# Copies of the first features for feature tiles that follow other work, and weight slots chosen by kind

## The chip, the core and the metric

One core of one Trainium2 chip runs the whole program. The metric is the device time of one execution in microseconds (us). The kernel before took 1661.35 us (median of three runs, 1661.29 to 1663.35).

## What is computed

Two transformer blocks on 256 tokens of width 1024, all in float32. The first is feed-forward, hybrid mixer (attention and a state-space scan), cross-attention on a memory, feed-forward; the second is another mixer and a feed-forward that picks 16 of 16384 experts for each of 8 heads and token.

```python
def first_block(x, mem, ...):
    f = swiglu(rmsnorm(h, ffn1_pre_g[l]), ffn1_w_gu[l], ffn1_w_down[l])
    h = h + 0.5 * rmsnorm(f, ffn1_post_g[l])
    m = hybrid_mixer(rmsnorm(h, mix_pre_g[l]), w_in[l], ...)
    h = h + rmsnorm(m, mix_post_g[l])
    c = memory_cross_attention(rmsnorm(h, xa_pre_g[l]), rmsnorm(mem, mem_g[l]), ...)
    h = h + rmsnorm(c, xa_post_g[l])
    f = swiglu(rmsnorm(h, ffn2_pre_g[l]), ffn2_w_gu[l], ffn2_w_down[l])
    return h + 0.5 * rmsnorm(f, ffn2_post_g[l])
...
def second_block(x, ...):
    proj = rmsnorm_2(x, norm_mix[l]) @ w_in[l]
    ...
    x = x + mix @ w_out[l]
    x = x + peer_ffn(rmsnorm_2(x, norm_ffn[l]), peer_wq[l], peer_keys[l], peer_u[l], peer_v[l])
    return rmsnorm_2(x, norm_f)
```

In `peer_ffn` the kernel multiplies the tokens by all rows of `peer_u`, builds the gates of the chosen experts as dense products of one-hot matrices, and multiplies by all rows of `peer_v`.

## The kernel before

**Units.** All weights come as 533 units of 512 KB, in one fixed list: `ff1` 66 units, `v` 8, `qk` 16, `dt` 1, `xs` 8, `bc` 4, `z` 8, `mk` 8, `wo1` 16, `mv` 8, `xq` 8, `xo` 8, `ff2` 66, `v2`, `g2`, `f2`, `q2` 4 each, `chb` 12, `wo2` 8, `pq` 16, `pu` 128, `pv` 128. SyncE loads a unit into a raw buffer. `prefetch` gives it a slot (a pair of 128x1024 tiles, `hi` and `lo`): ScalarE rounds the raw weights into `hi` (L156), VectorE writes the rest into `lo` (L157). This is called the split of a unit below. Weights and features are both kept as such a pair, so a product is three matmuls, high by high, low by high and high by low. `prefetch` is called from `tick` between pieces of TensorE's work, so a split stands in the queues of ScalarE and VectorE behind whatever was issued before it; the queues are served in order.

**Slots.** There are slots 0 to 3 (`hi0`/`lo0` to `hi3`/`lo3`), slots 4 to 7, and some more pairs taken out of the arenas `ra` and `fa` for a while by `extend`. Of the units in `HELD` each tile holds its weights still (see below); they get the lowest free slot, the others the highest. The addresses of the built program matter for the change: slots 0 to 3 start at 32 modulo 128 bytes; slots 4 to 7, the arenas and the feature buffers `uT` (high and low part) start at 96 modulo 128. In this text a matmul is *level* where its weights and its features have the same residue, and *off* where they are 64 bytes apart.

**Three kinds of matmuls take the units.** `f_tile` (L311, matmuls at L319, L320, L321) holds 128 columns of weights in TensorE and streams the 256 tokens of `uT`, 8 blocks k with three matmuls each; there are 277 such tiles, 6648 matmuls. `half_chunk` (matmuls at L286, L287, L290) and `acc_step` (L336, L338, L340) hold the features and stream 512 columns of weights. An f tile can be broken in its middle: after four blocks `tick` may let other generators put matmuls of attention, scans, transposes or gates in between. The other work is the transposes into `uT` (L397, then ScalarE L402 for the high part, VectorE L406 for the low part), attention (L599 to L636), the scans, and the gates of the experts (one-hot products, L1375) beside the tiles of `pu`.

**Order.** One Python program records all engines' instructions in one order, so each engine's queue follows from the order of the calls; a wait appears where data is needed.

**Where it stands in time** (us from the span's start): `ff1` to 190, first mixer with `v`, `qk`, `xs`, `bc`, `z`, `wo1` to 445, cross-attention to 530, `ff2` to 720, second mixer to 848, `pq` to 905, `pu` 905 to 1305 (gates beside it from 1032), `pv` to the end.

Of the kernel before, what the change touches and what calls it, by code (L numbers as in the profile page):

```python
# [110 lines left out]
class Builder:  # L111
    RAW = 3
    RING = (4, 4)
    VRING = 4

# [3 lines left out]
    def __init__(self, tc, io, dbg=None, stop=None):  # L119
# [11 lines left out]
        self.mm_i = self.sd_i = 0  # L131

# [8 lines left out]
    def prefetch(self, n=1):  # L141
# [130 lines left out]

    def half_chunk(self, u0, t, aT, evac, hook=None):
# [5 lines left out]
        for j in range(4):  # L279
# [3 lines left out]
            for kk in range(2):  # L283
                k = 2 * j + kk
                wh, wl = hi[:, kk * 512:kk * 512 + 512], lo[:, kk * 512:kk * 512 + 512]
                nc.tensor.matmul(ps, ah[:, k, ts], wh, start=(k == 0), stop=False)  # L286
                nc.tensor.matmul(ps, ah[:, k, ts], wl, start=False, stop=False)  # L287
            for kk in range(2):
                k = 2 * j + kk
                nc.tensor.matmul(ps, al[:, k, ts], hi[:, kk * 512:kk * 512 + 512], start=False, stop=(k == 7))  # L290
# [20 lines left out]
    def f_tile(self, u, aT, evac):  # L311

        nc = self.nc
# [14 lines left out]
    def acc_step(self, k, t, w, aT, first, last, halves=range(2)):  # L328
# [6 lines left out]
        for h in halves:  # L335
            nc.tensor.matmul(o[h], ah[:, k, ts], hi[:, hs[h]], start=first, stop=False)  # L336
        for h in halves:
            nc.tensor.matmul(o[h], ah[:, k, ts], lo[:, hs[h]], start=False, stop=False)  # L338
        for h in halves:
            nc.tensor.matmul(o[h], al[:, k, ts], hi[:, hs[h]], start=False, stop=last)  # L340
# [7 lines left out]
    def acc_gemm(self, u0, pairs, n, done=None, mid=None, tail=6, early=1, before_t1=None, have=None):  # L348
# [3 lines left out]
        for i, (aT, k, pos) in enumerate(pairs[:cut]):  # L352
# [3 lines left out]
            for t in range(2):  # L356
                self.acc_step(k, t, w, aT, pos == 0, pos == n - 1)
                if not t:
# [5 lines left out]
        for t in range(2):  # L364
            if t == 1 and before_t1:
                before_t1()
            for i, (aT, k, pos) in enumerate(pairs[cut:], cut):
# [5 lines left out]
                self.acc_step(k, t, self.get(u0 + i), aT, pos == 0, pos == n - 1)  # L373
                if t == 1:
# [14 lines left out]
    def transposes(self, src, t, dst, col=None, kt0=0, n=8, part=None):  # L389
# [4 lines left out]
        for b in range(0, n, 4) if part is None else [4 * part]:  # L394
            ps = self.sd()
            for i in range(4):
                nc.tensor.transpose(ps[:, i * 128:(i + 1) * 128],  # L397
# [79 lines left out]
    def ffn(self, name, row_name, before_t1, done, mid):  # L477
# [4 lines left out]
        if name != "ff1":  # L482
            self.extend(0, 4)
# [21 lines left out]
        def tr(c, ac):  # L505
            ps = self.sd()
            for j in range(2):
                for t in range(2):
                    nc.tensor.transpose(ps[:, j * 256 + t * 128:j * 256 + t * 128 + 128],
# [73 lines left out]
    def attention(self, par, qT, kT, vt, oat, ready):  # L583
# [10 lines left out]
        for j in range(4):  # L594
            while ready[0] <= j:
                yield
            for n in range(2):
                f = 2 * j + n
                nc.tensor.matmul(zv[:, n], kT[rows, f, 0:128], qT[rows, f, :], start=(n == 0), stop=False,  # L599
# [1200 lines left out]
```

## Time and profile before

| | |
|---|---|
| median of three runs | 1661.35 us |
| the profiled execution, its own time | 1661.53 us |
| its span in the trace | 1659.8 us |
| TensorE busy in the span | 1638.8 us, 99% |
| VectorE, ScalarE, GpSimd busy | 69%, 59%, 16% |

All sums below are made against 1661.5 us; the median lies 0.2 us lower. Times in the rows are microseconds from the start of the span. In a timeline row the first number is the start of the instruction, the second its duration; the matmuls overlap, so what one costs is read from the distance of the starts and not from the duration, which is 0.28 us for an f matmul throughout.

### The profile page before, as it was taken

The page shows a single profiled execution, that of the slowest core. Times are in us where ns is not written, and L with a number is a line of the kernel's source. Part 1 is how long each engine was busy: PE and PEld are TensorE (multiplying, and loading weights), DVE is VectorE, ACT ScalarE, POOL GpSimd, SP SyncE. Part 2 cuts the span into 40 slices and gives each one's busy share as a digit, 9 for nine tenths or more (in the row PEclk, how much of TensorE's full clock was granted, in tenths as well). Part 3 has the DMA queues.
Part 4 walks back from the last instruction along what each step waited for, and adds up shares of the span by engine and source line. Part 5 has one row for each costly group of instructions (what it writes and reads, how often), then busy time and mean ns, then how long its engine had stood idle before and what let it go on. Part 6 is the DMA issues. An engine that isn't in the chain of part 4 may idle for free.

```text
span 1659.8 us, 29155 instructions
## 1 busy us (share of the span) xinstructions
PE 1638.8 (99%) x11102; PEld 1490.7 (90%) x11102; DVE 1152.8 (69%) x2366; ACT 980.5 (59%) x1826; POOL 272.3 (16%) x311
## 2 busy tenths in 40 slices
PE   8999999999999999999999999999999999999998
PEld 6999899988898899989889999999999888888886
DVE  7555565777756755567657998899999755555554
ACT  7444476786555644456355564988877554455444
POOL 0000000000000000000100002988888100000000
PEclk9999999999999999999999999999999999999999
DMA  9555443364434755526234555444444555555553
GB/s 332 193 201 190 150 143 128 102 201 148 174 112 165 270 188 201 191 99 196 90 130 153 185 183 190 162 162 167 163 155 162 178 207 198 192 190 195 195 193 127
DMA packets 79325, 288.77 MB, mean 174 GB/s; under 512 B 8784, under 2 KB 8912, under 8 KB 79056
## 3 DMA queue, kind: packets, MB, share of 16 engines
q1 hardware_dynamic: 77904, 281.66, 49.3%
q10 hardware_dynamic: 1280, 5.24, 0.9%
q8 instruction: 87, 1.43, 0.3%
q14 instruction: 54, 0.44, 0.1%
HBM read 285.82 MB, written 1.05 MB: 173 GB/s over the span
## 4 chain that ended last, share of the span: by engine, by line
PE 89%; DVE 6%; issue 2%; ACT 1%; DMA 1%; POOL 0%; SPq 0%; POOLq 0%; DVEq 0%; ACTq 0%
PE mm L319 14%; PE mm L320 14%; PE mm L321 14%; PE acc L336 11%; PE acc L338 11%; PE acc L340 11%; PE mm L290 3%; PE mm L286 3%; PE mm L287 3%; DVE lo L157 2%; PE sd L1375 1%; DVE m L1365 1%; DMA raw<-ws 1%; DVE X L1385 1%; PE sd L397 1%
## 5 line engine op out<-in xcount | busy, mean ns | idle before, releaser
L157 DVE TENSOR_TENSOR lo<-raw,hi 128x1024 fp32r<-128x1024 f32 x419 | 513.7, 1230 | 262.4 <-ACT hi L156 261.2
L319 PE MATMUL mm<-uT,hi 128*128 128x256 f32 x2024 | 576.1, 285 | 3.3 <-ACT fa L1198 1.7
L156 ACT ACTIVATE hi<-raw 128x1024 fp32r<-128x1024 f32 x419 | 442.2, 1058 | 221.5 <-PE acc L340 185.6
L320 PE MATMUL mm<-uT,hi 128*128 128x256 f32 x2024 | 566.4, 280 | 0.0
L321 PE MATMUL mm<-uT,lo 128*128 128x256 f32 x2024 | 566.3, 280 | 0.0
L319 PEld LDWEIGHTS mm<-uT,hi 128*128 128x128 f32 x2024 | 381.5, 189 | 5.7 <-DVE X L1478 2.5
L320 PEld LDWEIGHTS mm<-uT,hi 128*128 128x128 f32 x2024 | 381.7, 189 | 0.8
L321 PEld LDWEIGHTS mm<-uT,lo 128*128 128x128 f32 x2024 | 381.2, 188 | 0.0
L1362 POOL TENSOR_SCALAR m<-iota,kT 128x128 f16<-128x128 f16 x256 | 235.3, 935 | 198.1 <-DVE kT L1345 151.9
L425 POOL TENSOR_TENSOR hr<-hv,mhalf 128x1 f32<-128x1 f32 x26 | 15.2, 585 | 816.4 <-DVE hv L424 816.4
L157 DVE TENSOR_TENSOR lo<-fa,hi 128x1024 fp32r<-128x1024 f32 x74 | 90.1, 1224 | 65.0 <-ACT hi L156 64.3
L338 PE MATMUL acc<-lo,r 128*128 128x512 f32 x336 | 103.5, 389 | 0.0
L336 PE MATMUL acc<-hi,r 128*128 128x512 f32 x336 | 103.4, 389 | 0.0
L340 PE MATMUL acc<-hi,r 128*128 128x512 f32 x336 | 103.4, 389 | 0.0
L156 ACT ACTIVATE hi<-fa 128x1024 fp32r<-128x1024 f32 x74 | 77.4, 1055 | 42.4 <-PE mm L320 23.5
L1475 ACT ACTIVATE X<-mm 128x256 f32<-128x256 f32 (+40 forms) x126 | 39.7, 315 | 99.9 <-PE mm L321 99.0
L1364 ACT ACTIVATE oh<-m,kT 128x128 f16<-128x128 f16 x256 | 81.1, 390 | 0.0
L338 PEld LDWEIGHTS acc<-lo,r 128*128 128x128 f32 x336 | 63.1, 188 | 13.1
L340 PEld LDWEIGHTS acc<-hi,r 128*128 128x128 f32 x336 | 63.1, 188 | 13.1
L336 PEld LDWEIGHTS acc<-hi,r 128*128 128x128 f32 x336 | 63.1, 188 | 13.0
L336 PE MATMUL acc<-hi,ra 128*128 128x512 f32 x216 | 71.0, 410 | 0.6 <-ACT ra L1183 0.6
L338 PE MATMUL acc<-lo,ra 128*128 128x512 f32 x216 | 67.3, 393 | 0.0
(364 smaller groups left out, 2653.2 us busy)
## 6 DMA issues: line engine op xcount, KB each, us to landing
raw<-ws SPq DMA_DIRECT2D x443, 512.0 KB, 3.3
fa<-ws SPq DMA_DIRECT2D x90, 512.0 KB, 3.6
fa<-rows ACTq DMA_DIRECT2D x5, 512.0 KB, 4.1
fa<-mem ACTq DMA_DIRECT2D x1, 1024.0 KB, 7.7
X<-keysT ACTq DMA_DIRECT2D x1, 1024.0 KB, 4.8
out<-X SPq DMA_DIRECT2D x4, 256.0 KB, 2.0
h<-x SPq DMA_DIRECT2D x2, 256.0 KB, 2.8
h<-x SPq DMA_DIRECT2D x1, 512.0 KB, 7.3
```

What stands on the lines that cost most here:

```text
L156: nc.scalar.activation(hi, raw, AF.Copy)
L157: nc.vector.tensor_sub(lo, raw, hi.bitcast(F32))
L286: nc.tensor.matmul(ps, ah[:, k, ts], wh, start=(k == 0), stop=False)
L287: nc.tensor.matmul(ps, ah[:, k, ts], wl, start=False, stop=False)
L319: nc.tensor.matmul(ps, wh, ah[:, k, :], start=(k == 0), stop=False)
L320: nc.tensor.matmul(ps, wh, al[:, k, :], start=False, stop=False)
L321: nc.tensor.matmul(ps, wl, ah[:, k, :], start=False, stop=(k == 7))
L336: nc.tensor.matmul(o[h], ah[:, k, ts], hi[:, hs[h]], start=first, stop=False)
L338: nc.tensor.matmul(o[h], ah[:, k, ts], lo[:, hs[h]], start=False, stop=False)
L340: nc.tensor.matmul(o[h], al[:, k, ts], hi[:, hs[h]], start=False, stop=last)
L1362: nc.gpsimd.tensor_scalar(m1[:, i], self.iota, key(0, i), None, op0=OP.is_equal)
L1364: nc.scalar.activation(oh[:, i], m1[:, i], AF.Copy, scale=key(2, i))
```

## The change

- `f_tile` keeps track of what TensorE did last (`last`: an f tile, other work, or a level token matmul). Where a tile, or the second part of a broken tile, follows something other than an f matmul and its unit is in slots 0 to 3 with `uT` as features, its first blocks take the features from copies instead of `uT`: three blocks after other work, one after a level token matmul. The copies `pr` hold blocks 0 and 1 of the high and low part at residue 32, the residue of slots 0 to 3; for `pq` and `pu` a third copy of the high part of block 2 is added. So six matmuls (eight in `pu`), or three, are level ahead of the off ones.
- `f_tile` issues high by high, low by high, high by low; a tile behind another f tile takes its blocks in the order 3, 4, 5, 6, 0, 1, 2, 7, so that after a break in the middle the copied blocks come next.
- GpSimd writes the copies in `spread`, two small copies for each 128 tokens, behind the writes of `uT`.
- `prefetch` gives units in `HELD` only slots 0 to 3 and the others only slots from 4 on. It takes a slot of the wrong kind only if the unit is fewer than three units ahead of the one in use. Units 4 to 7 of `mv` don't get arena slots. `extend(0, 4)` becomes `extend(0, 3)`; the arena `fa` shrinks from 16768 to 16128 floats for the copies.

```diff
+    AHEAD = 3
...
             slots = [x for x in self.free if x < self.RING[0] or i < FIRST["pq"]]
-            if not slots:
+            if FIRST["mv"] + 4 <= i < FIRST["mv"] + 8:
+                slots = [x for x in slots if x < sum(self.RING)]
+            fit = [x for x in slots if (x < self.RING[0]) == (i in HELD)]
+            if not fit and (i - self.top >= self.AHEAD and i < FIRST["pq"] or not slots):
                 return
-            slot = min(slots) if i in HELD else max(slots)
+            slot = max(fit or slots)
...
+    def level(self, i):
+
+        self.last = "level" if self.slot_of[i] >= self.RING[0] else "other"
...
-        for k in range(8):
+        lead, mine = 0, aT is self.uT and self.slot_of[u] < self.RING[0]
+        todo = list(range(8)) if self.last != "f" else [3, 4, 5, 6, 0, 1, 2, 7]
+        for n, k in enumerate(todo):
+            if self.last != "f":
+                lead = (0 if not mine else 1 if self.last == "level" else 3)
+                self.last = "f"
             wh, wl = hi[:, k * 128:k * 128 + 128], lo[:, k * 128:k * 128 + 128]
-            nc.tensor.matmul(ps, wh, ah[:, k, :], start=(k == 0), stop=False)
-            nc.tensor.matmul(ps, wh, al[:, k, :], start=False, stop=False)
-            nc.tensor.matmul(ps, wl, ah[:, k, :], start=False, stop=(k == 7))
-            if k == 3:
+            xh, xl = ((p[k] if k < lead and k < len(p) else x[:, k, :]) for p, x in zip(self.lead, aT))
+            nc.tensor.matmul(ps, wh, xh, start=(n == 0), stop=False)
+            nc.tensor.matmul(ps, wl, xh, start=False, stop=False)
+            nc.tensor.matmul(ps, wh, xl, start=False, stop=(n == 7))
+            if n == 3:
+                lead = 0
                 self.tick(1.3, False)
...
     def spread(self, hn, t, dst, col):
         self.transposes(hn[t].ap, t, dst, col)
+        ts = slice(t * 128, t * 128 + 128)
+        for p, x in zip(self.pr, dst):
+            self.nc.gpsimd.tensor_copy(p[:, :, ts], x[:, 0:2, ts])
         hn[t].free()
...
-            self.extend(0, 4)
+            self.extend(0, 3)
...
+        pr2 = px.tile([128, 256], F32R, name="pr2")
+        nc.gpsimd.tensor_copy(pr2, hT[0][:, 2, :])
+        self.lead[0].append(pr2)
...
+            self.pr = tuple(st.tile([128, 2, 256], F32R, name=f"pr{i}") for i in range(2))
+            self.lead = [[p[:, 0, :], p[:, 1, :]] for p in self.pr]
...
-    FN = 16768
+    FN = 16128
```

The order of TensorE's instructions is the same before and after, kind by kind and shape by shape; operands, slots and the places of the splits differ. On TensorE, in the middle of a tile of `pu` beside the gates, before (`uT0` and `uT1` are the high and low features, `hi3`/`lo3` slot 3):

```order
L1375 MATMUL sd0_75<-m2_10301,ol_10303 128x128
L319 MATMUL mm0_73<-uT0_90,hi3_87 128x256
L320 MATMUL mm0_73<-uT1_91,hi3_87 128x256
L321 MATMUL mm0_73<-uT0_90,lo3_88 128x256
L319 MATMUL mm0_73<-uT0_90,hi3_87 128x256
L320 MATMUL mm0_73<-uT1_91,hi3_87 128x256
L321 MATMUL mm0_73<-uT0_90,lo3_88 128x256
L319 MATMUL mm0_73<-uT0_90,hi3_87 128x256
L320 MATMUL mm0_73<-uT1_91,hi3_87 128x256
L321 MATMUL mm0_73<-uT0_90,lo3_88 128x256
```

The same place after:

```order
L1404 MATMUL sd0_75<-m2_10326,ol_10328 128x128
L341 MATMUL mm0_73<-pr0_89,hi3_87 128x256
L342 MATMUL mm0_73<-pr0_89,lo3_88 128x256
L343 MATMUL mm0_73<-pr1_90,hi3_87 128x256
L341 MATMUL mm0_73<-pr0_89,hi3_87 128x256
L342 MATMUL mm0_73<-pr0_89,lo3_88 128x256
L343 MATMUL mm0_73<-pr1_90,hi3_87 128x256
L341 MATMUL mm0_73<-pr2_7619,hi3_87 128x256
L342 MATMUL mm0_73<-pr2_7619,lo3_88 128x256
L343 MATMUL mm0_73<-uT1_93,hi3_87 128x256
```

Eight of these nine matmuls now read their features from the copies. On ScalarE, at the opening of `v`, from the end of the residual norm to the transposes of the second 128 tokens, before (`mm1`, `mm0` are results of token matmuls; the L156 rows are the splits of `v.7`, `qk.0` and `qk.1`):

```order
L430 ACTIVATE junk_1812,ssb_1807<-h_95 128x512
L833 ACTIVATE fa_108<-mm1_74 128x512
L156 ACTIVATE hi6_104<-fa_108 128x1024
L156 ACTIVATE hi4_100<-fa_108 128x1024
L156 ACTIVATE hi5_102<-fa_108 128x1024
L402 ACTIVATE uT0_90<-sd1_76,cols_77 128x128 x4
```

The same place after (L161 are the splits of `v.6`, `v.7`, `qk.0`, `qk.1`):

```order
L455 ACTIVATE junk_1817,ssb_1812<-h_97 128x512
L861 ACTIVATE fa_110<-mm1_74 128x512
L161 ACTIVATE hi5_104<-raw2_80 128x1024
L161 ACTIVATE hi4_102<-fa_110 128x1024
L161 ACTIVATE hi1_83<-fa_110 128x1024
L161 ACTIVATE hi0_81<-fa_110 128x1024
L427 ACTIVATE uT0_92<-sd1_76,cols_77 128x128 x4
```

The split of `v.6`, which stood ahead of the norm before, now stands behind the eviction of the token matmuls (L833, now L861). On ScalarE at the end of the first mixer, before (the splits in `ra` are `mv.0` and `mv.1`; `wo1.12` to `wo1.15` are further up):

```order
L791 ACTIVATE junk_3926,ss2_3925<-fa_108 128x512
L156 ACTIVATE ra_109<-raw1_79 128x1024
L156 ACTIVATE ra_109<-raw2_80 128x1024
L402 ACTIVATE uT0_90<-sd1_76,cols_77 128x128 x4
L402 ACTIVATE uT0_90<-sd0_75,cols_77 128x128 x4
```

The same place after (the splits in `ra` are `wo1.12` and `wo1.13`, those in `hi3` and `hi2` are `wo1.14` and `wo1.15`):

```order
L819 ACTIVATE junk_3924,ss2_3923<-fa_110 128x512
L161 ACTIVATE ra_111<-raw0_78 128x1024
L161 ACTIVATE ra_111<-raw1_79 128x1024
L427 ACTIVATE uT0_92<-sd1_76,cols_77 128x128 x4
L161 ACTIVATE hi3_87<-raw2_80 128x1024
L161 ACTIVATE hi2_85<-raw0_78 128x1024
L427 ACTIVATE uT0_92<-sd0_75,cols_77 128x128 x4
```

The last four units of `wo1` are split four places later than before, two of them between the transposes of the last features. VectorE's splits (L157) stand in the same places of its queue.

## Rows read from the trace of the kernel before

**Rows 1.** The page's first part: busy time, share and instructions of each engine.

```profile
PE 1638.8 (99%) x11102; PEld 1490.7 (90%) x11102; DVE 1152.8 (69%) x2366; ACT 980.5 (59%) x1826; POOL 272.3 (16%) x311
```

**Rows 2.** TensorE's timeline: start, duration, line, first and last L321 of three runs.

```profile
163.38 0.28 PE L321 MATMUL mm<-uT,lo 128*128 128x256 f32 x1
...
171.66 0.28 PE L321 MATMUL mm<-uT,lo 128*128 128x256 f32 x1
...
59.59 0.28 PE L321 MATMUL mm<-uT,lo 128*128 128x256 f32 x1
...
70.19 0.28 PE L321 MATMUL mm<-uT,lo 128*128 128x256 f32 x1
...
172.00 0.28 PE L321 MATMUL mm<-uT,lo 128*128 128x256 f32 x1
...
182.54 0.28 PE L321 MATMUL mm<-uT,lo 128*128 128x256 f32 x1
```

**Rows 3.** TensorE's timeline: a level half tile in slot 6 behind attention work.

```profile
283.84 0.28 PE L320 MATMUL mm<-uT,hi 128*128 128x256 f32 x1
...
285.03 0.28 PE L321 MATMUL mm<-uT,lo 128*128 128x256 f32 x1
```

**Rows 4.** TensorE's timeline: a level half tile behind attention, then an off tile.

```profile
330.57 0.36 PE L319 MATMUL mm<-uT,hi 128*128 128x256 f32 x1
...
331.96 0.28 PE L321 MATMUL mm<-uT,lo 128*128 128x256 f32 x1
...
332.31 0.28 PE L321 MATMUL mm<-uT,lo 128*128 128x256 f32 x1
...
340.13 0.28 PE L321 MATMUL mm<-uT,lo 128*128 128x256 f32 x1
```

**Rows 5.** Stretches: length, busy time (count) by engine, clock, DMA share, GB/s.

```profile
905.00:1009.00 104.00, 104.00 (x886) 104.00 (x885) 96.94 (x385) 61.15 (x92) 0.00 (x0) 1.00 0.55 185
...
1130.00:1230.00 100.00, 99.92 (x938) 98.61 (x938) 98.02 (x277) 81.85 (x215) 87.42 (x98) 1.00 0.48 159
1230.00:1302.00 72.00, 70.12 (x640) 67.90 (x639) 72.00 (x189) 51.96 (x143) 52.27 (x58) 1.00 0.46 155
```

**Rows 6.** Timelines of TensorE, ScalarE and VectorE at the opening of `v`.

```profile
206.88 0.39 PE L286 MATMUL mm<-ra,uT 128*128 128x512 f32 x1
...
208.47 0.39 PE L287 MATMUL mm<-lo,uT 128*128 128x512 f32 x1
...
207.70 2.94 ACT L156 ACTIVATE hi<-fa 128x1024 fp32r<-128x1024 f32 x3
...
208.84 3.49 DVE L157 TENSOR_TENSOR lo<-fa,hi 128x1024 fp32r<-128x1024 f32 x3
```

**Rows 7.** Timelines of TensorE and VectorE in `z`.

```profile
344.84 0.39 PE L287 MATMUL mm<-lo,uT 128*128 128x512 f32 x1
...
345.17 1.23 DVE L157 TENSOR_TENSOR lo<-raw,hi 128x1024 fp32r<-128x1024 f32 x1 [1.34 <-ACT hi L156]
```

**Rows 8.** Timelines of TensorE and VectorE at the opening of `g2`.

```profile
732.08 0.39 PE L287 MATMUL mm<-lo,uT 128*128 128x512 f32 x1
...
733.00 3.49 DVE L157 TENSOR_TENSOR lo<-fa,hi 128x1024 fp32r<-128x1024 f32 x3
```

**Rows 9.** Timelines of TensorE and VectorE at the end of `wo1`.

```profile
434.49 0.63 PE L338 MATMUL acc<-lo,uT 128*128 128x512 f32 x2
...
437.28 0.63 PE L338 MATMUL acc<-lo,uT 128*128 128x512 f32 x2
...
434.30 1.23 DVE L157 TENSOR_TENSOR ra<-raw,ra 128x1024 fp32r<-128x1024 f32 x1 [0.80 <-ACT ra L156]
...
436.98 1.12 DVE L406 SCALAR_TENSOR_TENSOR uT<-sd,cols,uT 128x128 fp32r<-128x128 f32 x4
```

**Rows 10.** TensorE and VectorE at the first tile of `xq`; GpSimd's group of L416.

```profile
469.60 0.28 PE L321 MATMUL mm<-uT,lo 128*128 128x256 f32 x1
...
468.90 2.16 DVE L406 SCALAR_TENSOR_TENSOR uT<-sd,cols,uT 128x128 fp32r<-128x128 f32 x8 [1.08 <-ACT uT L402]
...
L416 POOL TENSOR_SCALAR fa<-fa 128x1024 f32<-128x1024 f32 x2 | 6.6, 3321 | 192.5 <-DMA fa<-rows 99.5 <-ACT hi L156 93.0
```

More of the change, by code (lines that the diff above doesn't have):

```diff
@@ L131, in __init__ @@
         self.mm_i = self.sd_i = 0
+        self.last = "other"
     def load(self):
@@ L270, in sd, with pe @@
         return self.sdb[self.sd_i % 2]
+    def pe(self):
+        self.last = "other"
+        return self.nc.tensor
+    def level(self, i):
+        self.last = "level" if self.slot_of[i] >= self.RING[0] else "other"
     def half_chunk(self, u0, t, aT, evac, hook=None):
@@ L335, in acc_step @@
         for h in halves:
-            nc.tensor.matmul(o[h], ah[:, k, ts], hi[:, hs[h]], start=first, stop=False)
+            self.pe().matmul(o[h], ah[:, k, ts], hi[:, hs[h]], start=first, stop=False)
         for h in halves:
-            nc.tensor.matmul(o[h], ah[:, k, ts], lo[:, hs[h]], start=False, stop=False)
+            self.pe().matmul(o[h], ah[:, k, ts], lo[:, hs[h]], start=False, stop=False)
         for h in halves:
-            nc.tensor.matmul(o[h], al[:, k, ts], hi[:, hs[h]], start=False, stop=last)
+            self.pe().matmul(o[h], al[:, k, ts], hi[:, hs[h]], start=False, stop=last)
     def until(self, cond, but={}):
@@ L357, in acc_gemm @@
                 self.acc_step(k, t, w, aT, pos == 0, pos == n - 1)
+                self.level(u0 + i)
                 if not t:
@@ L679, in steps @@
         ps = self.sd()
-        nc.tensor.matmul(ps[:, 0:16], self.ident[:, 127:128].to_broadcast([128, 128]), dtk[:, 0, 1, :], start=True,
+        self.pe().matmul(ps[:, 0:16], self.ident[:, 127:128].to_broadcast([128, 128]), dtk[:, 0, 1, :], start=True,
                          stop=True)
@@ L778, in group @@
                     po = self.sd()
-                    nc.tensor.matmul(po, xp[:, 10 + g, 131:259], st[:, g], start=True, stop=True)
+                    self.pe().matmul(po, xp[:, 10 + g, 131:259], st[:, g], start=True, stop=True)
                     yo = mb[0].ap.rearrange("p (h q) -> p h q", h=8)
@@ L994, in values @@
                 for m in range(2):
-                    nc.tensor.matmul(ps, vm[:, m, f * 128:f * 128 + 128], pT[:, h, m, :], start=(m == 0),
+                    self.pe().matmul(ps, vm[:, m, f * 128:f * 128 + 128], pT[:, h, m, :], start=(m == 0),
                                      stop=(m == 1))
@@ L1061, in hgrn @@
         nc.scalar.activation(eb.ap, Gb.ap, AF.Exp)
-        dec = self.small.tile([128, 4, 8], F32, name="hdec", bufs=1)
+        decb = F.alloc(32)
+        dec = decb.v(h=4, n=8)
         nc.vector.tensor_copy(dec, e.rearrange("p h (n c) -> p h n c", c=32)[:, :, :, 31])
@@ L1157, in hgrn @@
             yield 0.23
-        for b in (keb, Ab, Sb):
+        for b in (keb, Ab, Sb, decb):
             b.free()
@@ L1483, in peer @@
             px.tile([128, self.PADS[4]], F32, name="pad4")
-        w01 = tuple(px.tile([128, 2, 256], F32R, name=f"w{i}") for i in range(2))
+        w01 = self.pr
         ring = []
@@ L1499, in peer @@
             early = i == 127 and self.g_done == 256
+            if i == 127:
+                self.lead = [[], []]
             if early:
@@ L1658, in keep @@
             for i in range(2):
[L1659 removed]
+                self.pe().matmul(self.acc[2 * t + i], self.ident, self.h[:, t, i * 512:i * 512 + 512], start=True,
                                  stop=False)
```

75 lines of the change are left out of this document (38 added, 37 removed).

## The prediction

> **What bounds the kernel.** I read the page first, then stretches, then TensorE's timeline. TensorE is busy for 1638.8 of 1659.8 us [rows 1]: the time is the sum of the distances between matmul starts, plus a few waits. VectorE is at 69% over the span, but that is a mean. While `pu` has the gates beside it VectorE works 98.02 of 100 and then 72.00 of 72 us, and TensorE has holes there (99.92 of 100, 70.12 of 72) [rows 5]. So a faster TensorE is worth its full gain in most of the program and little in the last part of the gates.
>
> The distances of the f matmuls take three values, though the printed duration is 0.28 us throughout [rows 2]. Three tiles in slots 4 to 6 (level): 163.38 to 171.66 is 69 matmuls, 120.0 ns each. Four tiles in slots 0 to 3 (off) that began behind token matmuls: 59.59 to 70.19, 90 matmuls, 117.8 ns. Four off tiles that began right behind level f tiles: 172.00 to 182.54, 93 matmuls, 113.3 ns. The granted clock is 1.00, its higher level of 2.4 GHz [rows 5], so it isn't the clock. The pace of an off tile depends on what ran before it, and it keeps this pace until other work breaks in: from 905 to 1009, with nearly nothing but off f matmuls, 886 matmuls take 104.00 us [rows 5], without a change of pace. Token matmuls differ by placement too: level 206.88 to 208.47, seven steps, 227 ns [rows 6]; off 434.49 to 437.28, twelve steps, 232.5 ns [rows 9].
>
> **Part 1, copies ahead of off tiles.** The change wants a few level matmuls ahead of every off run, so that it goes at 113.3 instead of 117.8 ns. By the addresses and the order, the 6648 f matmuls were 1728 level, 576 off at 113.3 and 4344 off at 117.8. After, all tiles are in slots 0 to 3: 837 level matmuls on copies; 5379 off behind such a lead; 432 without one (tiles whose features are not `uT`, and second parts of tiles whose order leaves no copied block). If every lead works: before 1728 x 0.1200 + 576 x 0.1133 + 4344 x 0.1178 = 784.3 us, after 837 x 0.1200 + 5379 x 0.1133 + 432 x 0.1178 = 760.8 us. From 23.5 I take off 1.0, since the first matmul of a piece behind other work takes about 0.2 us on either side of the change and belongs to neither pace: **22.5 us**. By stretch: `ff1` 4.0, `v` to `z` 1.9, to 565 0.6, `ff2` 3.6, second mixer 1.7, `pq` and `pu` without gates 5.5, `pu` with gates 5.2.
>
> Does a short lead work? A level half tile behind attention does: 12 level matmuls from 330.57 to 331.96, then 69 off steps from 332.31 to 340.13 at 113.3 ns [rows 4]. The change has 6, and 8 in `pu`. What the trace shows of fewer is the pace of the level run itself: from its second to its twelfth matmul one takes 119 ns on average (283.84 to 285.03, ten steps) [rows 3], so it is near its own 120 ns early, with single steps between 117 and 121 until the sixth to ninth. I take 0.5 off for starts behind the suffix sums of attention, where level runs settled latest.
>
> Bounds: all leads work, 22.5; only the leads of one block behind level token matmuls work (a level pace that is there already) 7.8 less 0.2; none works, and the matmuls that were at 113.3 lose that, minus 0.5.
>
> Here the Trainium skill speaks against the change. SBUF — State Buffer, "Who interferes with whom", gives TensorE two independent read ports, one for the moving operand and one for the weights, and says that "PE and ACT never wait on anyone". By that the residues of the two operands couldn't matter, part 1 would be worth nothing and the sum below would end slower, at the third rival's time. The trace differs: 113.3, 117.8 and 120.0 ns for the same shape at the same clock [rows 2].
>
> **Part 2, the slots.** Tiles move from slots 4 to 7 to 0 to 3 and token units the other way. 396 token matmuls become level, 108 become off: 288 x 5.8 ns = 1.7 us gained. What it costs is that each kind has its own slots and a unit is split only when one of its kind is free: the splits fall back in the queues, by the order most from some 20 to some 7 us of TensorE's work ahead of use. Most keep over 1.9 us. I put each split of after at the time at which the instructions around it ran before, and compare its end with the first matmul that reads it.
> - Opening of `v`: the split of `v.6` now stands first behind the eviction L833, where `v.7`'s stood. Its high part then ends at 207.70 + 1.05 and its low part at 208.84 + 1.22 = 210.06; TensorE reads it at 208.47 [rows 6]. Wait 1.6 us. Behind it TensorE has the transposes of the second 128 tokens, which were ready, so nothing is won back.
> - `ff2`'s opening has the same code and split order; I take the same 1.6.
> - `g2.2` at the opening of the second mixer: read at 732.08, low part done at 733.00 + 1.22 = 734.22 [rows 8], 2.1 us; VectorE has a normalization ahead of it.
> - `z.3`: read at 344.84, its place is that of a split that ended at 345.17 + 1.23 = 346.40 [rows 7], 1.6 us.
> - End of `wo1`: `wo1.12` is read at 434.49 and takes the place of the split that ended at 434.30 + 1.23 = 435.53, 1.0 us. `wo1.14` now stands behind the writes of `uT` that end at 436.98 + 1.12 = 438.10, so it ends at 439.3 and is read at 437.28: 2.0 us in all [rows 9].
> Together **8.9 us** of new waits. The lower bound is 0 (each queue catches up and the waits vanish, though I see no slack on ScalarE ahead of L833, which waits for TensorE itself); the upper, if each of these places waits for one more split of 1.2 us, 15.
>
> **Part 3, GpSimd's copies.** A copy of 2x128 columns has no row; L416, 1024 columns in 3.3 us, gives 0.8 us, with 0.3 and 1.5 as ends. Two copies behind each `spread` lie 5 us or more ahead of the first tile nearly everywhere. Not at `xq`: its first tile reads the low features at 469.60 while VectorE writes them from 468.90 [rows 10]. The copy can begin at about 469.55 and ends at 470.4, so TensorE waits some 0.8 us. The norms' GpSimd step (L425) stands behind the copies in that queue, 3 us later, and is covered.
>
> **Part 4, what comes late next.** In `pu` with gates VectorE leaves 2 us free in 100, then none [rows 5]; of the 3.3 us to win from 1130 to 1302 I keep 1.3, minus 2.0. In the second mixer a chain of ScalarE, VectorE and TensorE steps makes TensorE wait, so of 1.7 I estimate 1.0 lost. The rest is TensorE's own time up to the end.
>
> **The sum.** 22.5 + 1.7 - 0.5 - 8.9 - 0.8 - 2.0 - 1.0 = 11.0 us gained: 1661.5 - 11.0 = 1650.5 for an execution like the profiled one, **1650.3** as a median.
>
> **Rivals.**
> 1. *The late splits are hidden.* The whole program runs earlier, ScalarE and VectorE are idle a third of the time, and the places may shift. Then 8.9 + 0.8 come back: 1640.6. For it: a 99% busy TensorE shows how little waits today. Against: the split of `v.6` stands behind an eviction that waits for TensorE.
> 2. *Six matmuls are too few behind other work*, and only leads behind level token matmuls work. Then gains are 7.6 + 1.7 and losses 8.9 + 0.8 (those of part 4 don't arise): 1661.7, no change. For it: the level run's steps haven't settled by the sixth matmul, and in the long off run of `pu` no change of pace came by itself. Against: 12 matmuls did it with the same steps at the start [rows 4].
> 3. *No lead works, the slots cost all the same.* A few matmuls on copies don't set the pace, since it belongs to whole tiles or to other weights. (The rule of the Trainium skill above would end here too.) Gain 1.7 - 0.5, loss 9.7: 1670.0, slower. It decides against the change as soon as less than 8.0 of the 22.5 us arrive, about a third of the matmuls that are to change pace.
> 4. *A slot is short for longer*: units of f tiles have four slots and the others four or a few more, and the load of a raw buffer waits for a split. If that adds one split of 1.2 us in each of the 18 groups of `ff1` and `ff2`, 22 us come on top: 1672, slower. The splits in both loops keep over 2 us by the queue order, so I hold it unlikely.
>
> **Chances.** Forecast 0.57, rival 1 0.17, rival 2 0.13, rival 3 0.08, rival 4 0.05. A measurement of this kernel tells 0.2% (3.3 us) from no change, so faster is below 1658.0 and slower above 1664.7. The forecast and rival 1 are faster, and so is 0.02 of rival 2, if some leads of six work: 0.76. The rest of rival 2 is the same, 0.11; rivals 3 and 4 are slower, 0.13. The range takes the full hiding at its low end and rival 2 at its high end: 1640 to 1663; it leaves out rivals 3 and 4 and a little below.
>
> **What would show it.** Off tiles of `pu` without gates (905 to 1009 before) at 113.3 ns from one end to the other prove the lead: the stretch shrinks by 3.8 us. Off tiles at 113.3 ns behind the gates' products prove the lead of eight; at 117.8 rival 2 is right, and off tiles at 117.8 behind level token matmuls too would be rival 3. TensorE's waits by line should name splits (L161 or L162 of after) at `v.6`, `ff2.6`, `g2.2`, `z.3` and `wo1.12` to `wo1.14` with 1 to 2 us each; if they are absent rival 1 holds. I am wrong beyond the range if the leads fail at most places, or if the splits starve TensorE in the two feed-forward loops.

## The result, and the profile after

The kernel after takes 1685.95 us (median of four runs, 1685.68 to 1686.31) against 1661.39 us of the kernel before beside it: ratio 1.0145, interval 1.0128 to 1.0163. It is slower by 24.6 us; 11.0 us faster was forecast, and the range ended at 1663. The page of after, busy time, share and instructions of each engine:

```profile
PE 1650.3 (98%) x11102; PEld 1492.4 (89%) x11102; DVE 1145.9 (68%) x2366; ACT 975.1 (58%) x1826; POOL 286.1 (17%) x336
```

Beside [rows 1], TensorE is busy 11.5 us longer in a span that is 24.4 us longer: about one half is time in slower matmuls, the other idle time. TensorE's instructions stand in the same order in both kernels, so their starts can be compared one by one. How far after lies behind before grows like this (first column: time in the trace of before):

| stretch | growth |
|---|---|
| to 190 (`ff1`) | -0.8 us |
| 190 to 210 (opening of `v`) | +3.1 |
| 340 to 350 (`z`) | +1.6 |
| 430 to 470 (end of `wo1`, openings of `mv` and `xq`) | +7.5 |
| 530 to 550 (opening of `ff2`) | +5.1 |
| 720 to 760 (opening of the second mixer) | +2.6 -2.0 |
| 815 to 860 (its end) | +2.9 |
| all to 905, with smaller steps both ways | +18.4 |
| 905 to 1305 (`pu`) | 0.0 |
| 1305 to the end (`pv`) | +6.0 |

**`pu`: the leads set no pace.** The two stretches of [rows 5] that answer to `pu` without and with gates, moved by 18.4 us (length, busy time and count by engine, clock, DMA share, GB/s):

```profile
923.42:1027.42 104.00, 104.00 (x886) 104.00 (x885) 97.04 (x385) 60.91 (x92) 0.00 (x0) 1.00 0.58 184
1148.40:1248.40 100.00, 100.00 (x939) 98.83 (x939) 97.90 (x277) 81.90 (x215) 87.50 (x97) 1.00 0.50 159
```

886 matmuls in 104.00 us, exactly as before. TensorE's timeline at the first tile of `pu` shows the lead and what follows:

```profile
924.00 0.36 PE L341 MATMUL mm<-pr,hi 128*128 128x256 f32 x1
...
924.91 0.28 PE L342 MATMUL mm<-pr,lo 128*128 128x256 f32 x1
925.03 0.28 PE L343 MATMUL mm<-uT,hi 128*128 128x256 f32 x1
...
929.97 0.28 PE L343 MATMUL mm<-uT,hi 128*128 128x256 f32 x1
```

The eight matmuls on copies (`pr`) are there. Behind them 42 steps take 4.95 us (before the rounding of the rows), 117.8 ns each, where 113.3 was expected. The pace of 113.3 ns is gone from every tile on `uT`; the few steps of after that still have it are tiles on other features. Here are the f matmuls by the pace of their run (steps inside runs only, each run put to the nearest of the three paces):

| kernel | 120.0 | 117.8 | 113.3 | mean, ns |
|---|---|---|---|---|
| before | 1506 | 4270 | 569 | 117.91 |
| after | 237 | 6007 | 103 | 117.84 |

**The openings: waits.** TensorE's waits by the line that waited and what ended the wait (total, times, longest), after and then before:

```profile
PE sd L422 <- DVE fa L485: 14.1, 6, 6.7
PE mm L301 <- DVE lo L162: 3.8, 4, 1.3
PE mm L300 <- ACT hi L161: 0.8, 2, 0.6
```

```profile
PE sd L397 <- DVE fa L460: 6.7, 1, 6.7
```

The split waits that I forecast are there (L301 and L300). The larger part is another: transposes (L422) that wait for the normalized row block (L485), five new waits of 7.4 us in all. The one at the opening of `ff2`, in the timelines of ScalarE, VectorE and TensorE:

```profile
540.27 1.05 ACT L161 ACTIVATE hi<-raw 128x1024 fp32r<-128x1024 f32 x1
...
540.40 0.16 DVE L449 SCALAR_TENSOR_TENSOR hv<-ssa 128x1 f32<-128x1 f32 x1 [0.22 <-ACT junk L455]
541.35 1.23 DVE L162 TENSOR_TENSOR lo<-raw,hi 128x1024 fp32r<-128x1024 f32 x1 [0.79 <-ACT hi L161]
542.50 1.41 DVE L473 SCALAR_TENSOR_TENSOR h<-fa,hr,h 128x512 f32<-128x512 f32 x2
...
546.09 0.75 DVE L485 TENSOR_SCALAR fa<-h,hr 128x1024 f32<-128x1024 f32 x1 [1.09 <-POOL hr L450]
...
544.18 0.61 PE L363 MATMUL acc<-ra 128*128 128x512 f32 x2
546.90 1.35 PE L422 MATMUL sd<-ident,fa 128*128 128x128 f32 x8 [2.10 <-DVE fa L485]
```

A split that came earlier in the queues before now stands inside the chain of the norm: VectorE waits at 540.56 for the split's high part, then writes the low part, and the residual step L473 starts 2.1 us behind L449. In before there is nothing between the two:

```profile
528.75 0.16 DVE L424 SCALAR_TENSOR_TENSOR hv<-ssa 128x1 f32<-128x1 f32 x1
529.64 1.41 DVE L448 SCALAR_TENSOR_TENSOR h<-fa,hr,h 128x512 f32<-128x512 f32 x2 [0.73 <-POOL hr L425]
```

0.9 us there. And the wait costs more than itself: behind it TensorE runs at a lower granted clock for a while. Stretches of after (columns as above):

```profile
458.20:464.00 5.80, 5.80 (x23) 4.84 (x24) 5.80 (x12) 3.81 (x12) 1.19 (x2) 0.71 0.62 189
464.00:470.00 6.00, 6.00 (x28) 4.91 (x27) 3.98 (x8) 2.14 (x6) 1.10 (x2) 1.00 0.26 98
...
546.90:551.70 4.80, 4.80 (x18) 4.02 (x19) 4.28 (x10) 3.03 (x9) 1.37 (x2) 0.64 0.53 162
```

TensorE had been idle for 2.48 us ahead of the first and for 2.10 us ahead of the third. A mean of 0.71 or 0.64 is a part of the stretch at 1.2 GHz and the rest at 2.4. From the first transpose to the matmul fifteen instructions later it takes 4.13 us (458.15 to 462.28) and 4.12 us (546.90 to 551.02), in before 2.51 and 2.50: 1.6 us more each time. In stretches of 10 us, up to 1650 us in before and 1680 us in after, before has no such place and after only these two. How long TensorE was idle doesn't decide it alone: e1 below waits 2.11 us at the same opening (546.2) and keeps 1.00 from 546.2 to 551.0. So of `ff2`'s 5.1 us 2.2 come from the late transposes, 1.6 from the clock and 1.3 from one late split.

**`pv`: slower token matmuls.** TensorE's groups from 1400 to 1600 (count, busy, mean ns), before and then after; `r` and `pr` hold the features:

```profile
L338 PE MATMUL acc<-lo,r 128*128 128x512 f32 x198 | 61.0, 389 | 0.0
```

```profile
L361 PE MATMUL acc<-lo,r 128*128 128x512 f32 x194 | 60.8, 394 | 0.0
L361 PE MATMUL acc<-lo,pr 128*128 128x512 f32 x96 | 29.5, 389 | 0.0
```

By the distance of the starts, 1008 of `pv`'s matmuls, those on `r`, take 232.4 ns instead of 226.7: 5.8 us. The addresses of the two built programs differ here, which e2 below tests. The change also moves the 128-byte tile `hdec` into an arena; this edit was left out of the cut diff, because I gave it no price. Everything allocated behind it moves down by 128 bytes: `r` from 32 to 416 modulo 512, slots 4 to 7 and the arenas from 96 to 480. Modulo 128, the measure of the prediction, nothing has changed. From here on residues are modulo 512.

### The profile page after: what moved, and what is told of

Read it like the earlier page. It is cut to its first block, busy times and chain, and to the rows that moved or that the text cites. A ratio compares the mean times of both kernels' runs of the same rounds, so it can differ in the third digit from the quotient of the medians.

```text
span 1684.2 us, 29212 instructions
## 1 busy us (share of the span) xinstructions
PE 1650.3 (98%) x11102; PEld 1492.4 (89%) x11102; DVE 1145.9 (68%) x2366; ACT 975.1 (58%) x1826; POOL 286.1 (17%) x336
## 4 chain that ended last, share of the span: by engine, by line
PE 47%; DVE 7%; issue 1%; ACT 1%; POOL 0%; POOLq 0%; DVEq 0%; ACTq 0%
PE acc L359 7%; PE acc L361 7%; PE acc L363 7%; PE mm L341 7%; PE mm L342 7%; PE mm L343 7%; DVE lo L162 2%; DVE X L1414 1%; DVE m L1394 1%; PE sd L1404 1%; DVE ol L1396 1%; DVE X L1510 0%; PE mm L301 0%; PE sd L1462 0%; PE mm L304 0%
## 5 line engine op out<-in xcount | busy, mean ns | idle before, releaser
L161 ACT ACTIVATE hi<-raw 128x1024 fp32r<-128x1024 f32 x423 | 444.8, 1057 | 200.0 <-PE acc L363 179.5
L343 PE MATMUL mm<-uT,hi 128*128 128x256 f32 x1921 | 536.5, 279 | 0.0
L341 PE MATMUL mm<-uT,hi 128*128 128x256 f32 x1849 | 517.9, 280 | 0.0
L342 PE MATMUL mm<-uT,lo 128*128 128x256 f32 x1849 | 516.5, 279 | 0.0
L343 PEld LDWEIGHTS mm<-uT,hi 128*128 128x128 f32 x1921 | 360.3, 188 | 0.0
L341 PEld LDWEIGHTS mm<-uT,hi 128*128 128x128 f32 x1849 | 347.0, 188 | 0.1
L342 PEld LDWEIGHTS mm<-uT,lo 128*128 128x128 f32 x1849 | 346.9, 188 | 0.1
L162 DVE TENSOR_TENSOR lo<-fa,hi 128x1024 fp32r<-128x1024 f32 x64 | 77.5, 1224 | 44.2 <-ACT hi L161 44.1
L359 PE MATMUL acc<-hi,r 128*128 128x512 f32 x336 | 105.5, 395 | 0.0
L363 PE MATMUL acc<-hi,r 128*128 128x512 f32 x336 | 105.2, 394 | 0.0
L341 PE MATMUL mm<-pr,hi 128*128 128x256 f32 x303 | 93.6, 309 | 1.4 <-DVE X L1510 1.2
L546 ACT ACTIVATE fa<-mm 128x256 f32<-128x256 f32 x36 | 13.8, 384 | 138.5 <-PE mm L343 138.5
L342 PE MATMUL mm<-pr,lo 128*128 128x256 f32 x303 | 85.2, 281 | 0.0
```

The source lines that it names most:

```text
L161: nc.scalar.activation(hi, raw, AF.Copy)
L162: nc.vector.tensor_sub(lo, raw, hi.bitcast(F32))
L341: nc.tensor.matmul(ps, wh, xh, start=(n == 0), stop=False)
L342: nc.tensor.matmul(ps, wl, xh, start=False, stop=False)
L343: nc.tensor.matmul(ps, wh, xl, start=False, stop=(n == 7))
L359: self.pe().matmul(o[h], ah[:, k, ts], hi[:, hs[h]], start=first, stop=False)
```

## The experiments

Each kernel ran beside the kernel before (1660.5 to 1661.1 us). Where an experiment starts from another one, it is said.

**e1, after without leads.** What are the leads worth alone?

```diff
-                lead = (0 if not mine else 1 if self.last == "level" else 3)
+                lead = 0
```

> The changed kernel with no lead: every f tile reads uT from its first matmul, copies are written but not read; slots and addresses as in the changed kernel. Theory A (the leads set no pace, the loss of 24.5 us is slots and addresses): 1685 to 1686.5, f tiles at 117.8 ns as before. Theory B (the leads win something that the slots hide): slower by 5 us or more, 1691 and above. Theory C (the leads themselves cost): 1680 or less.

Measured 1683.0 us (two runs), ratio 1.0135 (1.0115 to 1.0156), beside after's 1.0145 (1.0128 to 1.0163): without the leads the kernel isn't slower. They win nothing. (Its trace is 1.5 us shorter than after's: 0.7 at `xq`, where TensorE no longer waits for the copies, and most of the rest at the opening of `ff2`, where its clock doesn't fall.)

**e2, after with the old residues.** Slots 4 to 7 and the arenas back to 96, `r` to 32; the third copy `pr2` is left out.

```diff
-    PADS = (0, 16, 16, 0, 0, 0)
+    PADS = (0, 16, 48, 0, 0, 32)
```

> The changed kernel with pads that bring slots 4 to 7, the arenas and the features of the last stage (r) back to the residues modulo 512 bytes that they had before (96, 96 and 32); the third copy pr2 is left out to make room. Theory A (the token matmuls of the last stage are slower because features and weights differ modulo 512, though they agree modulo 128): the last stage goes back from 231 to 226.7 ns and the whole to about 1679.5. Theory B (the residue modulo 128 decides, the last stage is slow for another reason, such as the buffers' order): 1685 to 1686.

Measured 1679.48 us (1677.06 to 1682.09), ratio 1.0119 (1.0102 to 1.0136). TensorE's groups in `pv` are back at 389 ns:

```profile
L361 PE MATMUL acc<-lo,r 128*128 128x512 f32 x196 | 60.3, 389 | 0.0
```

`pv` takes 347.96 us from its first to its last matmul, as before (347.97), where after takes 353.99. So 6.0 us of the 24.6 come from the 128 bytes.

**e3, only the new order of the three matmuls, in the kernel before.**

```diff
-            nc.tensor.matmul(ps, wh, al[:, k, :], start=False, stop=False)
-            nc.tensor.matmul(ps, wl, ah[:, k, :], start=False, stop=(k == 7))
+            nc.tensor.matmul(ps, wl, ah[:, k, :], start=False, stop=False)
+            nc.tensor.matmul(ps, wh, al[:, k, :], start=False, stop=(k == 7))
```

> The kernel before with the changed order of the three matmuls of a block alone (high by high, low by high, high by low). Theory A (the 113.3 ns pace behind level tiles needs the old order, in which the low features come second): the 576 matmuls at 113.3 go at 117.8, 1661.4 + 2.6 = 1664. Theory B (the order plays no part, the leads of the change are too short or of the wrong operand): 1661.4 and 113.3 ns stays.

Measured 1660.66 us, ratio 1.0001 (0.9991 to 1.0012). TensorE's timeline has both paces where before has them, first a level tile, then an off one:

```profile
167.88 0.28 PE L321 MATMUL mm<-uT,hi 128*128 128x256 f32 x1
...
171.12 0.28 PE L321 MATMUL mm<-uT,hi 128*128 128x256 f32 x1
...
172.17 0.28 PE L321 MATMUL mm<-uT,hi 128*128 128x256 f32 x1
...
181.01 0.28 PE L321 MATMUL mm<-uT,hi 128*128 128x256 f32 x1
```

27 steps of 120.0 ns, then 78 of 113.3. The order of the matmuls plays no part.

**e4, other pads in the kernel before.** `uT`, slots 4 to 7 and the arenas go to 480; slots 0 to 3 stay at 32, so that off weights now lie 64 bytes above the features (modulo 512) instead of 64 below.

```diff
-    PADS = (0, 16, 16, 0, 0, 0)
+    PADS = (0, 112, 16, 0, 32, 0)
```

> The kernel before with pads alone: uT, slots 4 to 7 and the arenas move by 384 bytes, so that the weights in slots 0 to 3 start 64 bytes above the features modulo 512 instead of 64 below; the last stage keeps its residues. Theory A (the distance modulo 512 with its sign sets the pace, as the tiles on other features at +64 in the changed kernel show with 113.3 ns without any lead): the 4344 matmuls at 117.8 ns go at about 113.3, 1661.4 - 19.5 = 1642, up to 1645 where VectorE or waits limit. Theory B (only what ran before sets the pace): 1661.4 within 1.5.

Measured 1650.42 us, ratio 0.9939 (0.9922 to 0.9955). The long run of `pu` goes at the fast pace without any lead (TensorE's timeline, 120 steps in 13.60 us, 113.3 ns):

```profile
923.07 0.28 PE L321 MATMUL mm<-uT,lo 128*128 128x256 f32 x1
...
936.67 0.28 PE L321 MATMUL mm<-uT,lo 128*128 128x256 f32 x1
```

But an off tile behind a level one is now slow, the reverse of before. From 162.16 to 170.80 it is level, 120.0 ns; then 81 steps from 171.86 to 181.40 take 117.8:

```profile
162.16 0.28 PE L321 MATMUL mm<-uT,lo 128*128 128x256 f32 x1
...
170.80 0.28 PE L321 MATMUL mm<-uT,lo 128*128 128x256 f32 x1
171.86 0.28 PE L321 MATMUL mm<-uT,lo 128*128 128x256 f32 x1
...
181.40 0.28 PE L321 MATMUL mm<-uT,lo 128*128 128x256 f32 x1
```

That, and off runs at 117.8 ns behind level token matmuls (shown with e9), is why the gain was half of what was expected. It also gives the next theory: not "level first" decides, but the direction in which an operand moves when the run turns off.

**e5 and e6, longer leads.** On e2, 12 and 24 level matmuls instead of 6; blocks 2 to 7 of a lead read the copies of blocks 0 and 1 again. The theories here: a lead of six is too short, or the lead fails because it changes the features and not the weights.

```diff
-                lead = (0 if not mine else 1 if self.last == "level" else 3)
+                lead = (0 if not mine else 8)
...
-            xh, xl = ((p[k] if k < lead and k < len(p) else x[:, k, :]) for p, x in zip(self.lead, aT))
+            xh, xl = ((p[k % 2] if k < lead else x[:, k, :]) for p, x in zip(self.lead, aT))
```

e6 also drops the `lead = 0` behind the fourth block, so a whole tile is level.

> The changed kernel with the restored residues of the run before, and leads of four blocks, twelve level matmuls, wherever an f tile or its second part follows other work. Only two blocks are copied, so the lead reads blocks 0 and 1 in place of 2 and 3: the products of these blocks are wrong, the work is the same. Theory A (a lead works when it is long enough for the level pace to settle at 120 ns): tiles behind a lead go at 113.3 ns, the long run of pu from 117.8 to 113.3, the whole 15 us or more below 1677. Theory B (a lead on copies never works, since it is the features and not the weights that change their residue at its end): 117.8 behind it, 1679 to 1681.

> As the run with twelve, but a tile that starts behind other work takes all eight blocks from the copies (24 level matmuls, blocks 2 to 7 replaced by blocks 0 and 1, so its products are wrong). Theory A (length): 113.3 ns behind it at least where the lead of twelve gives it. Theory B (the operand that changes): 117.8 ns behind 24 level matmuls too, though 24 and 48 level matmuls in slots 4 to 7 gave 113.3 before.

One run each: 1682.47 and 1684.57 us; their traces have two and four stretches at the lower clock where e2's has one, so the times say little and the pace decides. Behind the 12 of e5, 54 steps (927.51 to 933.87) take 117.8 ns. TensorE's timeline of e6 at the start of a lead tile in `pu`:

```profile
927.74 0.29 PE L343 MATMUL mm<-pr,hi 128*128 128x256 f32 x1
...
930.26 0.28 PE L343 MATMUL mm<-pr,hi 128*128 128x256 f32 x1
...
933.79 0.28 PE L343 MATMUL mm<-uT,hi 128*128 128x256 f32 x1
...
943.69 0.28 PE L343 MATMUL mm<-uT,hi 128*128 128x256 f32 x1
```

The lead goes at 120 ns (21 steps in 2.52 us), and the run behind it at 117.8 (84 steps in 9.89 us before rounding). Length is not what was missing.

**e7, the old choice of slots with the leads.** On e2; level tiles in slots 4 to 7 exist again.

```diff
-            fit = [x for x in slots if (x < self.RING[0]) == (i in HELD)]
-            if not fit and (i - self.top >= self.AHEAD and i < FIRST["pq"] or not slots):
+            if not slots:
                 return
-            slot = max(fit or slots)
+            slot = min(slots) if i in HELD else max(slots)
```

> The changed kernel with the restored residues and the old choice of slots (any free slot, lowest for f units, highest for the others); leads stay where a tile is in slots 0 to 3. Theory A (the 18 us that TensorE loses up to 860 us come from splits that stand late because each kind has its own slots): these waits go, and the time is 1660 to 1664. Theory B (the smaller arena, the copies on GpSimd or the shorter extension cause them): 1675 to 1680.

Measured 1660.74 us (eight runs), ratio 0.9996 (0.9986 to 1.0007): the 18.7 us between e2 and e7 (16.0 between their traces; e2's own runs lie 5 us apart) are the slots by kind. And one trace now holds both starts of an off run, behind a lead and behind a level tile:

```profile
59.61 0.28 PE L338 MATMUL mm<-pr,hi 128*128 128x256 f32 x1
...
60.20 0.28 PE L340 MATMUL mm<-uT,hi 128*128 128x256 f32 x1
...
70.80 0.28 PE L340 MATMUL mm<-uT,hi 128*128 128x256 f32 x1
...
116.39 0.28 PE L340 MATMUL mm<-uT,hi 128*128 128x256 f32 x1
...
121.49 0.28 PE L340 MATMUL mm<-uT,hi 128*128 128x256 f32 x1
```

Behind the lead 90 steps take 10.60 us, 117.8 ns: the features went up from 32 to 96. Behind the level tile 45 steps take 5.10 us, 113.3 ns: the weights went down from 96 to 32. Weights, features and shape of the off runs are the same.

**e8, everything 64 bytes the other way.** The kernel before with all slots at 32 and `uT` and `ra` at 480: no tile in slots 0 to 7 is level (those with weights in `ra` still are).

```diff
-    PADS = (0, 16, 16, 0, 0, 0)
+    PADS = (0, 112, 32, 112, 32, 0)
```

> The kernel before with pads alone: features uT and ra at 480 modulo 512, all slots 0 to 7 at 32, so that every f tile with uT has its weights 64 bytes above its features, and no tile in a slot is level; the last stage as before. Theory A (at +64 a start behind other work mostly finds 113.3 ns, and only level f tiles ahead of it spoil it): most f matmuls at 113.3, 1642 to 1647, below the run with +64 and level slots 4 to 7. Theory B (the level tiles of slots 4 to 7 cost nothing and token matmuls lose 3 ns each): 1650 to 1653.

Measured 1646.74 us, ratio 0.9914 (0.9898 to 0.9931): what the change was after, from pads alone. `pu` shrinks from 399.7 to 390.9 us. All its 3072 matmuls at 113.3 instead of 117.8 would give 13.8. A run of 192 from 998.99 that goes at 117.8 keeps 0.9 of the rest; the remainder is lost beside the gates, where VectorE has nothing left:

```profile
1130.00:1230.00 100.00, 99.11 (x946) 97.35 (x944) 100.00 (x281) 82.49 (x220) 91.39 (x99) 1.00 0.47 161
```

**e9, leads that go down.** On e7, with `uT`, slots 4 to 7 and the arenas at 480; the copies stay at 32.

```diff
-    PADS = (0, 16, 48, 0, 0, 32)
+    PADS = (0, 112, 48, 0, 0, 64)
...
-    FN = 16128
+    FN = 16000
```

> The changed kernel with the old choice of slots, restored residues of the last stage, and uT, slots 4 to 7 and the arenas at 480 modulo 512: weights in slots 0 to 3 lie 64 bytes above the features, and a lead on copies ends with the features moving down by 64. Theory A (behind level matmuls the pace depends on which operand moves and which way: weights down gave 113.3, features up 117.8, weights up 117.8; features down should give 113.3): nearly all tiles behind a lead at 113.3, about 1641 to 1646, below the 1650.4 of the same residues without leads. Theory B (a lead makes the pace behind it 117.8 whatever moves): tiles behind leads at 117.8, 1658 to 1662.

Measured 1650.13 us (two runs), ratio 0.9935 (0.9916 to 0.9955), the same as e4 (1650.42), which has these residues of `uT` and the slots and no leads. The pace is theory A's, the time is not. TensorE's timeline at one place of `ff1`, an off run behind level token matmuls, first e9 with a lead of three, then e4 without:

```profile
58.50 0.28 PE L338 MATMUL mm<-pr,hi 128*128 128x256 f32 x1
...
60.12 0.28 PE L340 MATMUL mm<-uT,hi 128*128 128x256 f32 x1
...
69.30 0.28 PE L340 MATMUL mm<-uT,hi 128*128 128x256 f32 x1
```

```profile
58.30 0.28 PE L321 MATMUL mm<-uT,lo 128*128 128x256 f32 x1
...
69.26 0.28 PE L321 MATMUL mm<-uT,lo 128*128 128x256 f32 x1
```

With the lead 81 steps take 9.18 us, 113.3 ns; without it 93 steps take 10.95 us (before rounding), 117.8 ns. A lead of this kind does work, but not for nothing: a run of 24 matmuls beside the gates that begins with one takes 2.86 us to the next instruction, one in e4 or e8 without 2.82, since these runs start at 113.3 by themselves. And the tiles of e9 in slots 4 to 7 are still level, and the off tiles behind them get no lead.

**e10, wrong-kind slots earlier.** e2 with one number changed.

```diff
-    AHEAD = 3
+    AHEAD = 8
```

> The changed kernel with restored residues and AHEAD 8 in place of 3: a unit takes a slot of the wrong kind already when it is fewer than eight units ahead of the one in use. Theory A (the waits come from splits held back for a slot of the right kind): most of the 18 us of waits go, 1660 to 1667 against 1679.5 with AHEAD 3. Theory B (the waits come from too few slots in all): 1677 to 1681.

Measured 1662.21 us (eight runs), ratio 1.0008 (0.9997 to 1.0018). The longest group of waits falls from 13.4 us in six waits (e2) to this:

```profile
PE sd L422 <- DVE fa L485: 8.5, 2, 7.3
```

The waits of e2 come from units that are held back for a slot of their kind, not from the slots themselves; of the larger steps over before only the 3.1 us at the end of the second mixer stay, made good elsewhere.

**e11, everything 256 apart.** The kernel before with all slots at 32 and features at 288. Does the residue modulo 512 decide, or a smaller one?

```diff
-    PADS = (0, 16, 16, 0, 0, 0)
+    PADS = (0, 64, 80, 64, 80, 0)
```

> The kernel before with pads alone: all slots at 32 modulo 512, uT and ra at 288, so features and weights are 256 bytes apart in every tile; the last stage as before. Theory A (the further apart modulo 512, the fewer collisions): f matmuls at 113.3 ns or less throughout, 1640 or below. Theory B (any distance other than 0 gives the same two paces, 113.3 and 117.8, by the start): between 1645 and 1661, with both paces in the trace.

Measured 1668.17 us, ratio 1.0043 (1.0029 to 1.0057); neither theory had this. TensorE's timeline in `pu`, 120 steps of 120.0 ns:

```profile
923.30 0.28 PE L319 MATMUL mm<-uT,hi 128*128 128x256 f32 x1
...
937.70 0.28 PE L319 MATMUL mm<-uT,hi 128*128 128x256 f32 x1
```

and token matmuls at 227 ns: 256 bytes apart is like level for both kinds. 128 apart is not for token matmuls (232.4 ns in `pv` of after); no run has f tiles 128 apart. So the residue modulo 256 fits all of these, and modulo 128 and 512 do not.

**e12, what the runs point to.** On e7: all slots at 32, `uT` and `ra` at 480, and leads of three blocks on every tile in slots 0 to 7 that starts behind other work ahead of `pu`, none in it.

```diff
-    PADS = (0, 16, 48, 0, 0, 32)
+    PADS = (0, 112, 48, 16, 0, 64)
...
-        lead, mine = 0, aT is self.uT and self.slot_of[u] < self.RING[0]
+        lead, mine = 0, aT is self.uT and self.slot_of[u] < sum(self.RING) and u < FIRST["pu"]
...
-                lead = (0 if not mine else 1 if self.last == "level" else 3)
+                lead = (3 if mine else 0)
```

(`ra` is also allocated ahead of slots 4 to 7, and `FN` is 16000.)

> All slots at 32 modulo 512 and the features uT and ra at 480 as in the run with all slots at +64, the old choice of slots, and leads of three blocks on copies at every start behind other work ahead of pu (none in pu, where starts at +64 mostly find 113.3 ns by themselves). Theory A (a level lead that ends with the features moving down always gives 113.3 ns): the tiles of both feed-forward loops and of the mixers behind a lead all at 113.3, and the time 1641 to 1645, below the 1646.7 without leads. Theory B (leads cost as much as they win, since a level matmul takes 119 to 120 ns): 1646 to 1649.

Measured 1643.61 us (1642.9 to 1644.1), ratio 0.9898 (0.9882 to 0.9915): the best of all, 16.9 us under the kernel before beside it. It lies 3.1 us under e8's median, but the intervals of the two ratios overlap, so by the times it isn't settled how much of it the leads give. The traces show them at work: the off runs of `ff1` that e8 begins behind level token matmuls at 75.30 and 158.80 go at 117.8 ns there and at 113.3 in e12 (from 75.27 and 158.36), and each feed-forward loop is 1.2 us shorter.

## Why the prediction was wrong, step by step

- **The leads, 22.5 us: the step that failed.** I read from [rows 4] that level matmuls ahead of an off run make it fast. In that row the weights change, down from 96 to 32, and the features stay. A copy changes the features, up from 32 to 96, and behind that e7 has 117.8 ns. I had named this possibility in rival 3 ("or to other weights") and gave the rival 0.08. The test was in my rows: the tiles at 113.3 ns in [rows 2] and [rows 4] stand behind a change of weights, none behind a change of features, so the 113.3 ns had no row for the operation that the change adds. My bound "none works" was the measured case. Counting steps, the mean of all f matmuls went from 117.91 to 117.84 ns, 0.4 us in all: the level tiles at 120.0 are gone, but so are the 113.3 ns behind them.
- **Six or twenty-four matmuls (rival 2).** Not the cause: e5 and e6.
- **Residue modulo 128.** I took "the same residue modulo 128" for level, because before has only residues 32 and 96. The 128 bytes that the change moves were invisible under it: 6.0 us in `pv` (e2), a term that my sum didn't have. The third copy `pr2` was built at 416, 128 from the slots modulo 256, so in `pu` two of the eight matmuls of a lead weren't level in this sense; e2, without it, has 117.8 ns all the same.
- **Late splits, 8.9 us with 15 as upper bound: the priced waits came, a larger one was put at nothing.** They came where I said. `v.6` waits (forecast 1.6 us):

```profile
209.29 0.50 PE L300 MATMUL mm<-hi,uT 128*128 128x512 f32 x1 [0.62 <-ACT hi L161]
...
210.60 0.51 PE L301 MATMUL mm<-lo,uT 128*128 128x512 f32 x1 [0.82 <-DVE lo L162]
```

  By the growth against before, `v.6` cost 2.0 us (forecast 1.6), `z.3` 1.6 (1.6), `g2.2` 2.0 (2.1), the end of `wo1` 2.2 (2.0) and `ff2.6` 1.3 (1.6): 9.1 in all, where I had 8.9. But the opening of `v` lost 3.1, the end of `wo1` to `xq` 7.5, and `ff2` 5.1. I priced only the matmul that reads the split. Not priced was what is queued behind the split on ScalarE and VectorE, the norm of the next stage (the five transposes that wait 7.4 us), nor the 1.6 us that the lower clock took twice. e7 and e10 give the whole term with these: 18.7 and 17.3 us.
- **`xq`, 0.8 us.** TensorE's timeline of after:

```profile
479.91 0.28 PE L342 MATMUL mm<-pr,lo 128*128 128x256 f32 x1
480.42 0.39 PE L343 MATMUL mm<-pr,hi 128*128 128x256 f32 x1 [0.23 <-POOL pr L497]
480.64 0.28 PE L341 MATMUL mm<-uT,hi 128*128 128x256 f32 x1
```

  A step of 0.51 and one of 0.22 us in place of 0.12 each, 0.5 us on GpSimd's copy; with the start of the tile it is 0.7 us against e1, which doesn't read the copies. The wait is as forecast, though a copy takes 0.40 us (median of 24) and not 0.8.
- **Token matmuls, 1.7 us gained.** Not seen: slots 4 to 7 came to lie 384 bytes from `uT`, 128 modulo 256, so this term had lost its ground as well.
- **Gates, 2.0 us, and the second mixer's chain, 1.0 us.** The first never arose, since nothing got faster; e8 shows it at work (VectorE 100.00 of 100, and 8.9 of 13.8 us arrive). The second mixer's end lost 2.9 us by waits of its own.
- **The outcome** is rival 3's: no lead works and the slots cost all the same. Its 1670.0 lacked 16 us: 6.0 of `pv`, and 18.4 where it had 9.7 less 1.2 gained. The rule of the Trainium skill that I set beside it (SBUF — State Buffer, "Who interferes with whom") ends at this time, but not for its reason: e8 and e11 differ in pads alone and lie 21.4 us apart, so the residues of the two operands do matter.

What stays open is why the direction counts. Behind token matmuls the traces of e4 and e8, with features 64 below the weights, show what sets the pace: all 15 off runs that start behind off token matmuls (229 to 233 ns) go at 113.3 ns, all 10 behind level ones (226.7 ns) at 117.8, as behind a level tile whose weights go up. Behind transposes, attention and the gates' products it stays open: with features 64 above such starts nearly always go at 117.8 ns, with features 64 below mostly at 113.3 in `pu`, and at either in attention. A lead that copies weights instead of features was not tried.

## What to carry to other kernels

A pace that follows some other work is worth building on only when a row shows it behind the very operand that the edit changes; a copy of the other operand is another experiment. When a rule holds work back until a better buffer is free, price everything queued behind that work, up to the next norm, and not only its reader. Compare the addresses of the built programs before and after, modulo more than the smallest measure that explains the old trace: 128 bytes moved by a tile that no one looked at cost a quarter of this loss, and pads alone gave 14 us.

## What the hardware showed unexpectedly

- An f matmul (128 held columns, 256 streamed) takes 120.0 ns where the operands' addresses agree modulo 256 and 113.3 or 117.8 where they are 64 bytes apart. A token matmul (512 streamed) is the other way round: 226.7 where they agree, 229 to 233 where they don't (64 or 128 apart modulo 256).
- Which of the two off paces a run gets depends on how it began. Behind a level run, weights going down by 64 bytes (e7) or features going down (e9) give 113.3; features going up (e6, e7) or weights going up (e4) give 117.8, behind level token matmuls too (e4, e8). The pace then holds for as long as nothing breaks in: 886 matmuls in 104.00 us.
- After idle times of 2.10 and 2.48 us the granted clock of after had fallen, and what followed cost 1.6 us more each time; around its shorter waits it stayed at 1.00. Other runs don't keep to that order: it stayed at 1.00 after 2.11 us in e1 (546.2), and fell after 0.82 us in e5 (0.66 from 211.5 to 216.5) and 1.21 us in e12 (0.64 from 793.2 to 798.0). So the same wait can cost 1.6 us more in one run than in another.
